# A two-layer hybrid encoder on Trainium2: gates after the second input tile, a normalisation without a DRAM turn, and three DMA queues

## The chip, the cores and the metric

The kernel runs on one core of a Trainium2 chip. The metric is the device time of one launch in microseconds (us). TensorE (PE) does the matrix products and transposes, VectorE (DVE), ScalarE (ACT) and GpSimd (POOL) do element-wise work, and DMAs are issued from an engine's own instruction stream: SyncE (SP) does nothing else, ACT and POOL issue them between their other instructions. PE writes its results to eight PSUM banks of 128 x 512 fp32.

## The reference

The input has 1024 tokens of width 1024; 16 learned tokens are put in front, so every activation is 1040 tokens long. Two layers follow, each a mixer and a SwiGLU FFN, with residual sums. The part that matters here is how the mixer gets its queries, keys, gates and decays:

```python
def l2norm(x):
    return x * lax.rsqrt(jnp.sum(x * x, axis=-1, keepdims=True) + L2_EPS)

def hybrid_mixer(h, ...):
    proj = h @ w_in
    qkv, z, b_raw, a_raw, sc_b, sc_c, sc_h = jnp.split(proj, idx, axis=-1)
    qkv = jax.nn.silu(depthwise_conv_centred(qkv, conv_qkv_w))
    q, k, v = jnp.split(qkv, 3, axis=-1)
    q = l2norm(q.reshape(Bsz, L, 4, 128))
    k = l2norm(k.reshape(Bsz, L, 4, 128))
    beta = jax.nn.sigmoid(b_raw).reshape(Bsz, L, 2, 4)
    g = -jnp.exp(a_log) * jax.nn.softplus(a_raw.reshape(Bsz, L, 2, 4) + dt_bias)
    o_fwd = chunk_gated_delta_rule(q, k, v, g[:, :, 0], beta[:, :, 0])
    o_bwd = flip(chunk_gated_delta_rule(flip(q), flip(k), flip(v), ...))
    ...
    y_sc = sc_b * depthwise_conv_centred(sc_c * sc_h, sc_conv_w)
    return jnp.concatenate([o * silu(z) ..., y_sc], axis=-1) @ w_out
```

Inside `chunk_gated_delta_rule` each chunk forms products of keys with keys and keys with queries, multiplies them by decays (exponentials of differences of the running sum of g), solves a triangular system, and a scan over the chunks carries a 128 x 128 state per head, forwards and backwards.

## The kernel before

**Layout.** Activations lie with features on the 128 partitions and tokens along the row: a tensor of 512 features is a tile `[128, 4, 1040]`. Every dense product is done in three matmuls for each 128 x 128 block of weights: high part by high part, high by low, low by high (L150, L151, L152 in `dense`). The weights arrive as fp32 (`raw`, L122, on SP's queue, 256 KB a transfer), ACT makes their high part `whi` (L123), and POOL, for some tiles DVE, their low part `wlo` (L124). There are three buffers each of `whi` and `wlo` and two of `raw`, so the next weights are fetched and split while PE works on the present ones.

**Order.** The program is written as straight Python loops for a scheduler that gives each instruction a priority and fixes one order for each engine before the run; `at_prio` moves parts of the code up or down. On the chip each engine follows its list and waits for semaphores. "Place" below means an instruction's position in that list of one engine. The list of SP holds all DMAs of the program, so a DMA that waits holds those behind it. Transfers also rotate over eight semaphores: each waits for the transfer eight before it on its kind of queue.

**A layer, in the order of the code:**

1. Input tiles (L405 to L434). `pos` 0 to 3 are the four heads of the keys (weight tiles 4 to 7), `pos` 4 to 7 those of the queries (tiles 0 to 3). Each tile is a dense product of 1024 x 128 weights with the 1040 tokens in three pieces `FULL` of 346 to 348 columns, a three-tap convolution, a SiLU and a square. The squares of a head are summed over their 128 features on PE, with a selecting matrix that puts head q into row q of a 32-row group, one group for each piece of columns (L425, bank `l2`).
2. `gates()` (L299), called at `pos == 6`, that is, at the third tile of the queries. It loads the small weights of beta and g, multiplies (L311, 48 matmuls), turns the result into tokens-on-partitions (L316), takes sigmoid and softplus through a chain of some 30 short DVE and ACT operations, sums g along the chunk on PE (L357, L358), transposes the sums (L361) and stores them to DRAM as `gd` (L364, on SP). It works in the tile `P0` (L305), and in three PSUM banks from `pa()`, which is a pool of one bank.
3. `normalise` (L376), for the keys behind `pos == 3` (with the tile `P1`) and for the queries behind `pos == 7` (with `P0`). The sums of four heads lie in 4 partitions by 1040 columns. ACT takes three square roots (L381), SP stores them to the DRAM buffer `rnd` (L382) and loads them back as 104 x 40 (L386), DVE takes the reciprocal (L387), SP stores it (L388), and for each head SP loads one row to all 128 partitions (L391) and DVE multiplies (L392). The tile for the queries is the `P0` that `gates` works in, so this load waits until the gates are done with it.
4. `k_out` (L394) transposes the keys and stores them for the scan (`vkd`, L403); value tiles follow, with transposes and stores in `v_store` (L463, L470, L472). Behind them stand the short convolution's twelve tiles and the four of z. Their matmuls have a low priority (`mmp`, `low`): they fill PE wherever the following parts leave room.
5. The chunk loop (L532): for each of nine chunks the products of keys with keys and with queries (L538, L539, banks `f` and `b`), for each direction a load of the rows of `gd` to all partitions (`gr`, L543), exponentials on ACT (L548, L552), products on DVE (L556, L560), a store for the scan (L562).
6. The triangular solve: 32 x 32 blocks on DVE and POOL (L603, L604), then joined on PE (L627 to L653).
7. The scan (`scan_step`, L673), nine chunks forwards and nine backwards, with dense filler between; then the output product and the FFN (L883 on).

Of the kernel before, what the change touches and what calls it, by code (L numbers as in the profile page):

```python
# [10 lines left out]
AF = mybir.ActivationFunctionType  # L11
# [7 lines left out]
H = 4  # L19
# [14 lines left out]
FULL = [(0, 348), (348, 694), (694, 1040)]  # L34
# [6 lines left out]
def trunk(ctx: ExitStack, tc: tile.TileContext, xT, w_in, w_ba, w_out, w_gu, w_dn,  # L41
          par_d, alog_d, dtb_d, cst_d, eye_d, out):
    nc = tc.nc
# [25 lines left out]
    def pa():  # L69
        return bank("a")  # L70
# [29 lines left out]
    ts = nc.vector.tensor_scalar  # L100
    ptt = nc.gpsimd.tensor_tensor
    dma = nc.sync.dma_start


    par = sb.tile([128, P_W], F32, name="par")
# [147 lines left out]
    for l in range(DEPTH):  # L253
# [45 lines left out]
        def gates():  # L299
# [7 lines left out]
            for (n0, n1) in FULL:  # L307
# [2 lines left out]
                    for j in range(2):  # L310
                        mm(ps[0:32, :n1 - n0], wb[:, k, :], x[k][j][:, n0:n1], start=(k == 0 and j == 0), stop=(k == 7 and j == 1))  # L311
                tt(out=bat[0:32, n0:n1], in0=ps[0:32, :n1 - n0], in1=rstd[0:32, n0:n1], op=ALU.mult)
            ps = pa()
            for c in range(9):
                s0 = 0 if c == 0 else 16 + 128 * (c - 1)
                mm(ps[:, c * 16:(c + 1) * 16], bat[0:32, s0:s0 + 128], sel2, start=True, stop=True)  # L316
# [34 lines left out]
            for d in range(2):  # L351
                tt(out=g[:, d], in0=sv[0][:, 36 * d:36 * d + 36].rearrange("p (c h) -> p c h", c=9),
                   in1=nA[:, 4 * d:4 * d + 4].unsqueeze(1).to_broadcast([128, 9, 4]), op=ALU.mult)
                ts(out=g[:, d, 0, :], in0=g[:, d, 0, :], scalar1=mask16, scalar2=None, op0=ALU.mult)
            psG = pa()
            for d in range(2):
                mm(psG[:, 36 * d:36 * d + 36], (utri, ltri)[d], fl(g)[:, 36 * d:36 * d + 36], start=True, stop=True)  # L357
            mm(psG[:, 72:144], ones, fl(g), start=True, stop=True)  # L358
            ts(out=fl(negG), in0=psG[:, 0:72], scalar1=-1.0, scalar2=None, op0=ALU.mult)
            psT = pa()  # L360
            nc.tensor.transpose(psT[0:72, 0:128], fl(negG), ident)  # L361
            grows = gt[0:72, 2, 0:128]
            nc.vector.tensor_copy(grows, psT[0:72, 0:128])
# [12 lines left out]
        def normalise(dst, l2, r, tag):  # L376

            scale, bias = ((float(HD), epsq), (1.0, epsc))[r > 0]
            r4 = row(Y[1] + "f")[0:4]
            for j, (n0, n1) in enumerate(FULL):  # L380
                act(out=r4[:, n0:n1], in_=l2[32 * j:32 * j + 4, :n1 - n0], func=AF.Sqrt, scale=scale, bias=bias[32 * j:32 * j + 4])  # L381
            dma(rnd[r:r + 4], r4)  # L382

            flat = rnd[r:r + 4].rearrange("a (b c) -> (a b) c", c=40)
            r104 = row(Y[1] + "f")[0:104, 0:40]
            dma(r104, flat)  # L386
            nc.vector.reciprocal(out=r104, in_=r104)  # L387
            dma(flat, r104)  # L388
            bc = big(tag)
            for h in range(H):  # L390
                dma(bc[:, h, :], rnd[r + h].partition_broadcast(128))  # L391
                tt(out=dst[:, h, :], in0=dst[:, h, :], in1=bc[:, h, :], op=ALU.mult)  # L392

        def k_out(c):  # L394

            n = 16 if c == 0 else 128
            s0 = 0 if c == 0 else 16 + 128 * (c - 1)
            ps = pa()
            for h in range(H):
                nc.tensor.transpose(ps[0:n, h * 128:(h + 1) * 128], KTt[:, h, s0:s0 + n], ident)  # L400
            kt = t2k("kt")
            act(out=kt[0:n].rearrange("p a b -> p (a b)"), in_=ps[0:n], func=AF.Copy)
            dma(vkd[c, 0:n, 1, :], kt[0:n].rearrange("p a b -> p (a b)"))  # L403

        for pos, i in enumerate((4, 5, 6, 7, 0, 1, 2, 3)):  # L405
            hh = pos % 4
            if hh == 0:
                l2, squares = None, []
            t = trow()
            late = pos < (2, 1)[l]  # L410
            inproj(i, to_row_late(t) if late else to_row(t), pfirst if l == 0 and pos == 1 else None)
            if late:
                tt(out=t, in0=t, in1=rstd, op=ALU.mult)
            dst = (QT if i < 4 else KTt)[:, hh, :]
            conv(t, dst, P_CV + 3 * i)
            act(out=dst, in_=dst, func=AF.Silu)
            act(out=t, in_=dst, func=AF.Square)

            squares.append((hh, t))
            if l > 0 or pos > 0:  # L420
                if l2 is None:
                    l2 = bank("f")
                for (q, sq_) in squares:
                    for j, (n0, n1) in enumerate(FULL):
                        mm(l2[32 * j:32 * j + 32, :n1 - n0], sel[:, 3 - q:35 - q], sq_[:, n0:n1], start=(q == 0), stop=(q == 3), skip_group_check=True)  # L425
                squares = []
            if pos == 6:
                beta, g, negG, negE, gl, bkd = gates()
            if pos == 3:
                normalise(KTt, l2, 4, "P1")  # L430
            if pos == 5:
                for c in range(9):
                    k_out(c)
# [24 lines left out]
        def v_store(i, v):  # L458

            for c0 in (0, 1, 5):  # L460
                ps = pa()
                if c0 == 0:
                    low(lambda: nc.tensor.transpose(ps[0:16, 0:128], v[:, 0:16], ident))  # L463
                    nc.vector.tensor_copy(vm[0:16, i, :], ps[0:16, 0:128])
                    if i == 3:
                        dma(vkd[0, 0:16, 0, :], vm[0:16].rearrange("p a b -> p (a b)"))
                else:
                    vt = v[:, 16 + 128 * (c0 - 1):16 + 128 * (c0 + 3)]
                    for c in range(4):
                        low(lambda: nc.tensor.transpose(ps[:, c * 128:(c + 1) * 128], vt[:, 128 * c:128 * c + 128], ident))  # L470
                    act(out=vt, in_=ps, func=AF.Copy)
                    dma(vkd[c0:c0 + 4, :, 0, i * 128:(i + 1) * 128].rearrange("c p e -> p c e"), vt.rearrange("p (c e) -> p c e", c=4))  # L472

        v = None
        for i in range(4):
# [56 lines left out]
        for c in range(9):  # L532
            n = 16 if c == 0 else 128
            s0 = 0 if c == 0 else 16 + 128 * (c - 1)
            kqp = [bank("fb"[c % 2]) for _ in range(2)]
            for h in range(H):
                o = (h % 2) * 256
                mm(kqp[h // 2][0:n, o:o + n], KTt[:, h, s0:s0 + n], KTt[:, h, s0:s0 + n], start=True, stop=True)  # L538
                mm(kqp[h // 2][0:n, o + 128:o + 128 + n], KTt[:, h, s0:s0 + n], QT[:, h, s0:s0 + n], start=True, stop=True)  # L539
            for d in (dirs0 if c == 0 else (0, 1)):  # L540
                pn[0] += 1
                gr, dt_, eg = pts[pn[0] % 4], pts[4 + pn[0] % 2], pts[6 + pn[0] % 2]
                dma(gr[:, :, 0:n], gd[36 * d + 4 * c:36 * d + 4 * c + 4, 0:n].partition_broadcast(128))  # L543
                aq = c4k("aq")
                at = aq[:, 0:512].rearrange("p (h i) -> p h i", h=4)
                qd = aq[:, 512:1024].rearrange("p (h i) -> p h i", h=4)
                if c > 0 or d == 1:
                    act(out=eg[:, :, 0:n], in_=gr[:, :, 0:n], func=AF.Exp, scale=-1.0)  # L548
                    tt(out=qd0 if c == 0 else qd, in0=QT[:, :, s0:s0 + n], in1=eg[:, :, 0:n], op=ALU.mult)
                ptt(out=gr[0:n, :, 0:n], in0=gr[0:n, :, 0:n], in1=off[0:n, d, 0:n].unsqueeze(1).to_broadcast([n, 4, n]), op=ALU.add)  # L550
                for h in range(H):
                    act(out=dt_[0:n, h, 0:n], in_=gr[0:n, h, 0:n], func=AF.Exp, scale=-1.0, bias=negG[0:n, d, c, h:h + 1])  # L552
                for j in range(2):
                    qk = kqp[j].rearrange("p (a b i) -> p a b i", a=2, b=2)[0:n, :, 1, 0:n]
                    o_ = at0[d][:, 2 * j:2 * j + 2, :] if c == 0 else at[:, 2 * j:2 * j + 2, :]
                    tt(out=o_, in0=qk, in1=dt_[0:n, 2 * j:2 * j + 2, 0:n], op=ALU.mult)  # L556
                for h in range(H):
                    o = (h % 2) * 256
                    dst = P0[d][:, h, :] if c == 0 else Pv[d][:, (c - 1) * 4 + h, :]
                    stt(out=dst, in0=kqp[h // 2][0:n, o:o + n], scalar=beta[0:n, d, c, h:h + 1], in1=dt_[0:n, h, 0:n], op0=ALU.mult, op1=ALU.mult)  # L560
                if c > 0:
                    dma(aqd[c, d].rearrange("p a b -> p (a b)"), aq[:, 0:1024])  # L562
                else:

                    Wm, Zm, Tm = mts
                    dma(m0d[d, 0].rearrange("h j i -> j h i"), P0[d])
                    dma(Wm, m0d[d, 0])
                    dma(Zm, eye_d[0:4, :, :][:, 0:16, 0:16])
                    for s in (range(15, 0, -1) if d == 0 else range(0, 15)):
                        r0, r1, a0, a1 = (0, s, s, 16) if d == 0 else (s + 1, 16, 0, s + 1)  # L570
                        sh = [4, r1 - r0, a1 - a0]
                        ptt(out=Tm[:, r0:r1, a0:a1], in0=Wm[:, r0:r1, s:s + 1].to_broadcast(sh), in1=Zm[:, s:s + 1, a0:a1].to_broadcast(sh), op=ALU.mult)
                        ptt(out=Zm[:, r0:r1, a0:a1], in0=Zm[:, r0:r1, a0:a1], in1=Tm[:, r0:r1, a0:a1], op=ALU.subtract)
                    dma(m0d[d, 1], Zm)
                    dma(P0[d], m0d[d, 1].rearrange("h j i -> j h i"))
# [677 lines left out]
```

## Time and profile before

| | before |
|---|---|
| timed executions | 2670.06, 2680.13, 2682.99 us |
| median | 2680.13 us |
| the profiled execution's own time | 2667.47 us |
| its span | 2665.7 us |
| mean granted PE clock over it | 0.983 |
| layer 0: tiles of keys, queries and the first of values | 50 to 174 us |
| layer 0: chunk loop; solve; scan | 174 to 250; 250 to 336; 336 to 560 us |
| layer 1: the same four | 1350 to 1517; 1517 to 1594; 1594 to 1670; 1670 to 1900 us |

The span runs from the first to the last instruction; the profiled execution's time is 1.8 us more. Times of instructions are microseconds from the span's start. The windows of the table were cut by hand where one stage's main instructions give way to the next stage's; the filler runs across these cuts. In a row of a timeline the columns are start, duration, engine, line, operation and the program's names of the destination and the source, with a count where several run back to back, and in brackets how long the engine was idle before and what ended that. In a row of a group they are line, engine, operation, names, count, shortest, median and longest duration in ns, and the start of the first and of the last in us. "SPq" is SP's queue of DMA issues: the duration is that of the issue, not of the transfer. Names such as `P`, `b`, `pf` stand for a tile's tag without its number: `P` is `P0` or `P1`, `pa`, `pf`, `pb`, `pacc` are PSUM banks.

### The profile page before, as it was taken

The page shows a single profiled execution, that of the slowest core. Times are in us where ns is not written, and L with a number is a line of the kernel's source. Part 1 is how long each engine was busy: PE and PEld are TensorE (multiplying, and loading weights), DVE is VectorE, ACT ScalarE, POOL GpSimd, SP SyncE. Part 2 cuts the span into 40 slices and gives each one's busy share as a digit, 9 for nine tenths or more (in the row PEclk, how much of TensorE's full clock was granted, in tenths as well). Part 3 has the DMA queues.
Part 4 walks back from the last instruction along what each step waited for, and adds up shares of the span by engine and source line. Part 5 has one row for each costly group of instructions (what it writes and reads, how often), then busy time and mean ns, then how long its engine had stood idle before and what let it go on. Part 6 is the DMA issues. An engine that isn't in the chain of part 4 may idle for free. (4 is left out here: it accounts for less than half of the span.)

```text
span 2665.7 us, 43982 instructions
## 1 busy us (share of the span) xinstructions
PE 2563.4 (96%) x17242; PEld 2346.7 (88%) x17242; DVE 1502.8 (56%) x2258; ACT 1032.8 (39%) x1932; POOL 1185.1 (44%) x922
## 2 busy tenths in 40 slices
PE   8998899999999999999999989999989999999997
PEld 7898899998999999999998977898877888887886
DVE  7369713548766566522353688135587766754216
ACT  5466334535333333321244662535343333332224
POOL 4136611224766666533221346112367666663342
PEclk9999889999999999999999999999999999999998
DMA  3246135634312222532222461356332222225321
GB/s 118 98 148 201 49 103 185 193 105 135 104 60 84 80 73 76 198 111 65 76 92 86 125 229 50 125 179 230 99 124 93 68 82 77 87 88 185 93 81 64
DMA packets 163491, 301.03 MB, mean 113 GB/s; under 512 B 20352, under 2 KB 57140, under 8 KB 163284
## 3 DMA queue, kind: packets, MB, share of 16 engines
q1 hardware_dynamic: 163284, 298.23, 34.2%
q8 instruction: 135, 2.21, 0.4%
q14 instruction: 72, 0.59, 0.1%
HBM read 222.99 MB, written 75.18 MB: 112 GB/s over the span
## 5 line engine op out<-in xcount | busy, mean ns | idle before, releaser
L124 POOL TENSOR_TENSOR wlo<-raw,whi 128x512 fp32r<-128x512 f32 x236 | 285.8, 1214 | 927.9 <-ACT whi L123 812.1
L150 PE MATMUL pacc<-a,whi 128*128 128x346 f32 (+2 forms) x1031 | 350.0, 342 | 10.6 <-ACT whi L123 6.1
L152 PE MATMUL pacc<-a,wlo 128*128 128x346 f32 (+2 forms) x1031 | 351.0, 342 | 6.8 <-DVE wlo L124 6.7
L123 ACT ACTIVATE whi<-raw 128x512 fp32r<-128x512 f32 (+2 forms) x264 | 151.7, 578 | 478.9 <-PE pacc L151 300.6
L151 PE MATMUL pacc<-a,whi 128*128 128x346 f32 (+2 forms) x916 | 313.2, 342 | 1.8 <-DVE a L799 1.7
L152 PE MATMUL pacc<-b,wlo 128*128 128x346 f32 (+2 forms) x882 | 303.3, 345 | 8.2 <-DVE wlo L124 8.2
L150 PE MATMUL pacc<-b,whi 128*128 128x346 f32 (+2 forms) x882 | 305.5, 347 | 4.2 <-ACT whi L123 2.1
L151 PE MATMUL pacc<-b,whi 128*128 128x346 f32 (+2 forms) x776 | 268.6, 347 | 0.7 <-DVE b L799 0.6
L150 PEld LDWEIGHTS pacc<-a,whi 128*128 128x128 f32 x1031 | 199.0, 194 | 21.7 <-ACT whi L123 6.5
L152 PEld LDWEIGHTS pacc<-a,wlo 128*128 128x128 f32 x1031 | 199.7, 194 | 16.5 <-DVE wlo L124 8.0
L151 PEld LDWEIGHTS pacc<-a,whi 128*128 128x128 f32 x916 | 177.3, 194 | 10.6 <-DVE a L799 2.0
L150 PEld LDWEIGHTS pacc<-b,whi 128*128 128x128 f32 x882 | 168.2, 191 | 20.1 <-issue 4.2
L152 PEld LDWEIGHTS pacc<-b,wlo 128*128 128x128 f32 x882 | 168.1, 191 | 19.2 <-DVE wlo L124 9.5
L942 POOL TENSOR_TENSOR wlo<-rw,whi 128x512 fp32r<-128x512 f32 x92 | 135.5, 1475 | 71.2 <-ACT whi L941 65.6
L151 PEld LDWEIGHTS pacc<-b,whi 128*128 128x128 f32 x776 | 147.9, 191 | 11.2 <-DVE b L799 1.6
L942 POOL TENSOR_TENSOR a<-rw,a 128x512 fp32r<-128x512 f32 x64 | 107.1, 1676 | 66.5 <-ACT a L941 66.4
L942 POOL TENSOR_TENSOR b<-rw,b 128x512 fp32r<-128x512 f32 x64 | 90.5, 1418 | 83.9 <-ACT b L941 52.3
L804 DVE TENSOR_TENSOR a<-pacc,a 128x346 f32<-128x346 f32 (+2 forms) x116 | 57.7, 500 | 108.3 <-PE pacc L152 107.1
L941 ACT ACTIVATE whi<-rw 128x512 fp32r<-128x512 f32 x92 | 58.0, 632 | 140.1 <-DVE rw L1015 72.5
L804 DVE TENSOR_TENSOR b<-pacc,b 128x512 f32<-128x512 f32 (+1 forms) x88 | 52.6, 599 | 99.2 <-PE pacc L152 98.9
L1011 DVE TENSOR_TENSOR rw<-rw,rw 128x512 f32<-128x512 f32 x44 | 68.5, 1556 | 49.3 <-POOL wlo L942 31.0
L1016 DVE TENSOR_TENSOR rw<-raw,rw 128x512 f32<-128x512 f32 x44 | 95.3, 2165 | 1.2
(822 smaller groups left out, 7504.3 us busy)
## 6 DMA issues: line engine op xcount, KB each, us to landing
raw<-in_w_in SPq DMA_DIRECT2D x112, 256.0 KB
raw<-in_w_gu SPq DMA_DIRECT2D x104, 256.0 KB
rw<-in_w_gu SPq DMA_DIRECT2D x88, 256.0 KB
aqd<-aq SPq DMA_DIRECT2D x32, 512.0 KB
rec<-aqd SPq DMA_DIRECT2D x62, 256.0 KB
rec<-vkd SPq DMA_DIRECT2D x61, 256.0 KB
raw<-in_w_dn SPq DMA_DIRECT2D x60, 256.0 KB
raw<-in_w_out SPq DMA_DIRECT2D x48, 256.0 KB
```

The costliest lines, as they stand in the source:

```text
L123: act(out=hi, in_=raw[:, 0:kk, :], func=AF.Copy)
L124: (tt if lov[0] else ptt)(out=lo, in0=raw[:, 0:kk, :], in1=hi.bitcast(F32), op=ALU.subtract)
L150: mm(ps[:, :n], wh, xh[:, n0:n1], start=(k == 0), stop=False)
L151: mm(ps[:, :n], wh, xl[:, n0:n1], start=False, stop=False)
L152: mm(ps[:, :n], wl, xh[:, n0:n1], start=False, stop=(k == K - 1))
L804: tt(out=hr[m][:, n0:n1], in0=ps, in1=hr[m][:, n0:n1], op=ALU.add)
L941: act(out=hi, in_=src, func=AF.Copy)
L942: ptt(out=lo, in0=src, in1=hi.bitcast(F32), op=ALU.subtract)
L1011: tt(out=s1t, in0=A21, in1=A22, op=ALU.add)
L1016: tt(out=A21, in0=A11, in1=A21, op=ALU.subtract)
```

## The change

There are three parts.

- The gates are called at `pos == 2`, the third tile of the keys, and their three PSUM banks come from the pool `b` of two banks, which the chunk loop and the solve use later.
- `normalise` sums the squares in four groups of 260 columns, so that they fill the 128 partitions in four groups of 32. One square root and one reciprocal work on 128 x 260 in place. Each head's four pieces are then stored to its row of `rnd` and loaded to all partitions by DMAs that POOL issues (`qdma`): eight a call, 32 in all.
- The stores of the transposed keys (18) and values (16) and the loads of the gates' rows (35) are issued by ACT (`adma`) instead of SP.

All else is the same source; the scheduler makes its lists anew.

```diff
@@ -102,2 +102,4 @@
     dma = nc.sync.dma_start
+    adma = nc.scalar.dma_start
+    qdma = nc.gpsimd.dma_start
 
@@ -312,3 +314,3 @@
                 tt(out=bat[0:32, n0:n1], in0=ps[0:32, :n1 - n0], in1=rstd[0:32, n0:n1], op=ALU.mult)
-            ps = pa()
+            ps = bank("b")
             for c in range(9):
@@ -354,3 +356,3 @@
                 ts(out=g[:, d, 0, :], in0=g[:, d, 0, :], scalar1=mask16, scalar2=None, op0=ALU.mult)
-            psG = pa()
+            psG = bank("b")
             for d in range(2):
@@ -359,3 +361,3 @@
             ts(out=fl(negG), in0=psG[:, 0:72], scalar1=-1.0, scalar2=None, op0=ALU.mult)
-            psT = pa()
+            psT = bank("b")
             nc.tensor.transpose(psT[0:72, 0:128], fl(negG), ident)
@@ -378,15 +380,10 @@
             scale, bias = ((float(HD), epsq), (1.0, epsc))[r > 0]
-            r4 = row(Y[1] + "f")[0:4]
-            for j, (n0, n1) in enumerate(FULL):
-                act(out=r4[:, n0:n1], in_=l2[32 * j:32 * j + 4, :n1 - n0], func=AF.Sqrt, scale=scale, bias=bias[32 * j:32 * j + 4])
-            dma(rnd[r:r + 4], r4)
-
-            flat = rnd[r:r + 4].rearrange("a (b c) -> (a b) c", c=40)
-            r104 = row(Y[1] + "f")[0:104, 0:40]
-            dma(r104, flat)
-            nc.vector.reciprocal(out=r104, in_=r104)
-            dma(flat, r104)
+            r4 = row(Y[1] + "f")[:, 0:260]
+            act(out=r4, in_=l2[:, 0:260], func=AF.Sqrt, scale=scale, bias=bias)
+            nc.vector.reciprocal(out=r4, in_=r4)
+            for h in range(H):
+                qdma(rnd[r + h].rearrange("(a c) -> a c", a=4), r4.rearrange("(a b) c -> a b c", b=32)[:, h, :])
             bc = big(tag)
             for h in range(H):
-                dma(bc[:, h, :], rnd[r + h].partition_broadcast(128))
+                qdma(bc[:, h, :], rnd[r + h].partition_broadcast(128))
                 tt(out=dst[:, h, :], in0=dst[:, h, :], in1=bc[:, h, :], op=ALU.mult)
@@ -402,3 +399,3 @@
             act(out=kt[0:n].rearrange("p a b -> p (a b)"), in_=ps[0:n], func=AF.Copy)
-            dma(vkd[c, 0:n, 1, :], kt[0:n].rearrange("p a b -> p (a b)"))
+            adma(vkd[c, 0:n, 1, :], kt[0:n].rearrange("p a b -> p (a b)"))
 
@@ -423,6 +420,6 @@
                 for (q, sq_) in squares:
-                    for j, (n0, n1) in enumerate(FULL):
+                    for j, (n0, n1) in enumerate([(260 * j, 260 * j + 260) for j in range(4)]):
                         mm(l2[32 * j:32 * j + 32, :n1 - n0], sel[:, 3 - q:35 - q], sq_[:, n0:n1], start=(q == 0), stop=(q == 3), skip_group_check=True)
                 squares = []
-            if pos == 6:
+            if pos == 2:
                 beta, g, negG, negE, gl, bkd = gates()
@@ -471,3 +468,3 @@
                     act(out=vt, in_=ps, func=AF.Copy)
-                    dma(vkd[c0:c0 + 4, :, 0, i * 128:(i + 1) * 128].rearrange("c p e -> p c e"), vt.rearrange("p (c e) -> p c e", c=4))
+                    adma(vkd[c0:c0 + 4, :, 0, i * 128:(i + 1) * 128].rearrange("c p e -> p c e"), vt.rearrange("p (c e) -> p c e", c=4))
 
@@ -542,3 +539,3 @@
                 gr, dt_, eg = pts[pn[0] % 4], pts[4 + pn[0] % 2], pts[6 + pn[0] % 2]
-                dma(gr[:, :, 0:n], gd[36 * d + 4 * c:36 * d + 4 * c + 4, 0:n].partition_broadcast(128))
+                adma(gr[:, :, 0:n], gd[36 * d + 4 * c:36 * d + 4 * c + 4, 0:n].partition_broadcast(128))
                 aq = c4k("aq")
```

## The prediction

> **What bounds the kernel now.** I read the page first, then the busy times by stretch, then the waits of TensorE (PE), then the SP and VectorE (DVE) timelines around the normalisation of the queries. A line such as L391 is a line of the kernel before.
>
> ```profile
> span 2665.7 us, 43982 instructions
> ...
> PE 2563.4 (96%) x17242; PEld 2346.7 (88%) x17242; DVE 1502.8 (56%) x2258; ACT 1032.8 (39%) x1932; POOL 1185.1 (44%) x922
> ...
> q1 hardware_dynamic: 163284, 298.23, 34.2%
> ```
>
> PE is busy 96% of the span, so at most 102 us of idle can be won anywhere. All transfers of the program itself run on one hardware queue; none on a queue fed by GpSimd (POOL). The stretches, layer 0 and then layer 1, each as input tiles of K, Q and first V, then chunk loop, then block solve, then scan:
>
> ```profile
> core 0: us, PE busy (x) PEld busy (x) DVE busy (x) ACT busy (x) POOL busy (x), PEclk, DMA share, GB/s
> 50.00:174.00 124.00, 123.63 (x801) 113.43 (x800) 63.60 (x94) 65.15 (x84) 26.06 (x19) 0.99 0.30 96
> 174.00:250.00 76.00, 66.71 (x443) 63.95 (x444) 64.34 (x153) 49.96 (x112) 51.21 (x79) 0.98 0.68 219
> 250.00:336.00 86.00, 75.38 (x832) 72.30 (x831) 68.06 (x104) 32.31 (x41) 52.04 (x72) 0.92 0.20 68
> 336.00:560.00 224.00, 218.02 (x1795) 209.00 (x1792) 87.21 (x216) 97.48 (x292) 37.48 (x25) 0.95 0.49 159
> 1350.00:1517.00 167.00, 166.88 (x1065) 154.10 (x1063) 76.53 (x119) 77.64 (x102) 31.24 (x24) 0.99 0.28 92
> 1517.00:1594.00 77.00, 67.89 (x410) 61.82 (x409) 67.29 (x152) 54.82 (x115) 40.29 (x48) 0.98 0.68 218
> 1594.00:1670.00 76.00, 66.67 (x587) 56.48 (x587) 63.72 (x94) 22.12 (x28) 49.56 (x69) 0.93 0.17 56
> 1670.00:1900.00 230.00, 227.84 (x1890) 206.56 (x1885) 91.50 (x211) 98.39 (x284) 45.53 (x32) 1.00 0.50 162
> ```
>
> The stretch with the code that moves (50 to 174, and 1350 to 1517) has no idle to give: 0.37 and 0.12 us. In the chunk loops and solves PE loses 9.29 + 10.62 + 9.11 + 9.33 = 38.35 us, with DVE 79 to 87% busy; in the scans 5.98 + 2.16 us. What PE waits for from 160 to 350 is not the chain of the attention but its dense filler work:
>
> ```profile
> engine line waited for: us in total, times, longest us
> PE pacc L152 <- DVE wlo L124: 6.7, 3, 4.2
> PE pa L463 <- ACT b L471: 4.4, 1, 4.4
> PE pb L538 <- DVE P L560: 2.9, 3, 1.3
> ```
>
> The low parts of weights split on DVE, and copies of V, come late because they stand in DVE's and ACT's queues among the chunk loop and the solve. Only the third row belongs to the chain.
>
> **The wait that the change takes away.** SP's timeline around the query normalisation, in layer 0 (layer 1 has the same order):
>
> ```profile
> 147.75 0.30 SPq L388 DMA_DIRECT2D rnd<-b3f  x1
> 148.15 10.45 SPq L122 DMA_DIRECT2D raw<-in_w_in  x3
> 160.90 0.32 SPq L364 DMA_DIRECT2D gd<-P  x1
> 162.38 1.86 SPq L391 DMA_DIRECT2D P<-rnd  x4
> ```
>
> The reciprocal is stored at 147.75, but its broadcast leaves at 162.38, 1.48 us after the store of the gates (L364): it needs the buffer P0 that the gates hold, and stands behind them on SP. So gates after tile 2 release the broadcast, not the missing DRAM turn alone. PE did not stand still meanwhile (0.37 us idle).
>
> **Cost, part by part.** The last sums of squares of Q, the square roots with their table loads and a reciprocal over 128 by 260, each from the groups of its line:
>
> ```profile
> L425 PE MATMUL pf<-b,sel x48: 454/467/481, 62.9 to 138.2; 128*32 128x346 f32 x32, 128*32 128x348 f32 x16
> ```
>
> ```profile
> L381 ACT ACT_TABLE_LOAD  x4: 1283/1283/1283, 76.0 to 1481.0; - x4
> ...
> L381 ACT ACTIVATE b3f<-pf,epsq x3: 542/542/542, 140.2 to 141.3; 4x346 f32<-4x346 f32 x2, 4x348 f32<-4x348 f32 x1
> ```
>
> ```profile
> L192 DVE RECIPROCAL r<-r x3: 1740/1767/1778, 674.9 to 1984.8; 128x260 f32<-128x260 f32 x2, 128x256 f32<-128x256 f32 x1
> ```
>
> The products with the broadcast, from DVE's timeline:
>
> ```profile
> 166.45 3.50 DVE L392 TENSOR_TENSOR b<-b,P 128x1040 f32<-128x1040 f32 x2 [1.81 <-DMA P<-rnd]
> ...
> 170.90 2.38 DVE L392 TENSOR_TENSOR b<-b,P 128x1040 f32<-128x1040 f32 x2
> ```
>
> In the built order of the program before, these sums stand at PE's places 292 to 751, which is (138.2 - 62.9)/459 = 0.164 us a place. Let T be the end of the last of them, and p the time that POOL needs to issue one transfer. Normalisation: one square root instead of three (0.6 us, the table load ahead of it), a reciprocal of 1.77 us (nothing waits on DVE there: 63.60 of 124 us busy): T + 2.4. Then POOL in its built order: four stores, a low part, four broadcasts, a low part. The low parts of layer 0's stretch and what POOL waited for ahead of them, then the broadcasts' issues on SP:
>
> ```profile
> L124 POOL TENSOR_TENSOR wlo<-raw,whi x17: 1278/1289/2385, 50.3 to 166.4; 128x512 fp32r<-128x512 f32 x17
> ...
>   ACT whi L123: 101.1, 15
> ```
>
> ```profile
> L391 SPq DMA_DIRECT2D P<-rnd x16: 326/426/549, 84.2 to 1505.8; - x16
> ```
>
> The broadcasts leave from T + 2.4 + 4p + 1.3; the first lands 166.45 - 162.38 = 4.1 us later, and the fourth product ended 10.9 us after the issue (170.90 + 2.38 - 162.38). The trace has no POOL transfer. The nearest rows are an SP issue of 0.43 us below and a two-input POOL operation of 1.29 us, at its longest 2.4, above; I take p = 1, nearer the POOL operation, and 0.4 to 2.4 as its ends. Then the first query product begins at T + 11.8 = 150.0 instead of 166.45, and all end at T + 18.6 = 156.8 instead of 173.28: the chain starts 16 us earlier. PE's first query product moves from place 935 to 866, which is 69 places or 11.3 us; 109 places behind the sums it is reached at T + 17.9, so it hardly waits.
>
> What this does to PE is in the low parts behind the broadcasts. For Q the last is done at T + 2.4 + 4p + 1.3 + 4p + 1.3 = T + 5 + 8p, and PE needs it 69 places, 11.3 us, behind: 1.7 us late at p = 1, none at 0.79 and below, 12.9 at 2.4. For K there is the same sum, and the need comes 89 places, 14.6 us, behind: none at 1, 9.6 at 2.4. POOL waits for ACT 101 us in this stretch, so its time is free; its order is not. Both layers: 3.4 us, between 0 and 45.
>
> Gates: their matmuls move to places 220 to 267, before the fourth tile, with the same instructions and other PSUM banks. Before, no PE wait came of them. Their DVE chain:
>
> ```profile
> 138.00 0.20 DVE L329 COPY beta<-pa 128x36 f32<-128x36 f32 x1 [2.22 <-PE pa L316]
> ...
> 152.44 0.36 DVE L354 TENSOR_SCALAR g<-g,misc 128x4 f32<-128x4 f32 x2
> ```
>
> That is 14.8 us, with other tiles' work inside; PE now comes to the sums over g (L357) 68 places, 11.2 us, after the last L316. So 3.6 us late a layer at worst, 0 if less stands between: I take 1.5, 3.0 in all. The sums of squares go from three to four matmuls with the same 1040 columns: 4 x 0.467 x 260/346 = 1.40 = 3 x 0.467, nothing.
>
> ACT takes 69 transfers off SP (18 of K, 16 of V, 35 of the gate rows) and four table loads more (5.1 us). The same issues cost SP:
>
> ```profile
> L403 SPq DMA_DIRECT2D vkd<-kt x18: 319/327/1004, 100.0 to 1474.9; - x18
> ```
>
> ```profile
> L543 SPq DMA_DIRECT2D ptm<-gd x35: 319/338/2007, 164.3 to 1567.7; - x35
> ```
>
> At 0.33 us the 51 in the chunk loops are 8.4 us a layer on an ACT that is busy 49.96 of 76: hidden in its idle time. If that cover is gone, the V copies are later, and the 4.4 us wait of L463 grows. Every transfer also waits for the one eight before it in the built order, so ACT can now be held by SP's stores; SP in turn carries less. Nothing is charged for either, 19 us at the upper end (third rival).
>
> The head start I price at 2 us of gain, out of the 8.14 us of scan idle: filler remains behind the scan in the built order, and the chunk loop spans 311 places of PE after, 303 before, the solve starting 367 behind it against 372. So the crowding that makes the 38.35 us moves along with the chain. Sum: 3.4 + 3.0 - 2 = +4.4 us, 2671.9 on the profiled execution's own 2667.47. That execution lies 12.7 us under the median 2680.13 of the three timed ones; the middle of all four is 2675.1, so I predict 2680. About 0.5%, 13.4 us, is what a measurement can tell from no change.
>
> **Rivals.** *POOL is slow to issue.* One transfer takes p = 2, as DVE's two-input operations already stretch POOL's 1.29 us to 2.39. Then Q costs 21 - 11.3 = 9.7 and K 21 - 14.6 = 6.4 us a layer, 32 in all, and with the gates 2675 + 35 = 2710. It decides for slower from p = 1.3. For it: DVE is in use beside every transfer; against: 26.06 of 124 us of POOL are busy there. [...]
>
> *The chain gains what it starts earlier.* With 16 us more, DVE is less crowded from 174 to 336, and half of the 38.35 us of PE idle goes: -19 us, 2656. It decides from an idle of 25 us in the four stretches; with 27 us of it gone the time is 2648. For it: only 63.60 of 124 us of DVE are busy in the stretch into which the chain moves; against: the wait rows name filler.
>
> *ACT becomes the crowded queue.* Table loads, issues and waits hold V's copies, and the idle of the four stretches grows by half: +19 us, 2694.
>
> *Nothing moves:* the broadcasts still leave late, held by something else than the gates: 2675.
>
> **How the numbers follow.** Forecast 0.33, nothing moves 0.03, slow POOL 0.28, crowded ACT 0.10, gain 0.26. Faster by over 0.5%: 0.26; same: 0.36; slower: 0.38. The range runs from the gain's farther end, 2648, to the slow POOL at p = 2.3, which makes 12.1 + 8.8 us a layer and 2720; it leaves out under a tenth at each end, where p is over 2.3 or yet more of the idle goes. The forecast's own range is 2667 to 2693.
>
> **What would show it.** Right: the broadcasts of Q leave about 9 us after the last sum of squares, the first chunk product of Q comes 11 us or more earlier, PE waits under 3 us a layer for low parts on POOL, and the idle of the chunk loops and solves together stays near 38 us. Wrong: POOL's transfers of 1.4 us and more with PE waiting on wlo from POOL; an idle of those stretches under 25 or over 52 us; a granted clock there that differs by more than 0.03, which no step here foresees.

## The result and the profile after

Over 22 runs the changed kernel took 2691.81 us (median, 2676.84 to 2703.77), the kernel before 2677.24 us over 22 runs: a ratio of 1.0053, with a 95% interval of 1.0035 to 1.0071. It is slower by some 14 us; forecast was 2680, no change. The gates now stand behind the third input tile (`pos == 2`), not the second as the title has it, and the normalisation keeps one of its two turns through DRAM. Lines below are those of the changed kernel: up to the gates they stand 2 later than before, behind the normalisation 3 earlier.

The page of the changed kernel, its head and its queues:

```profile
span 2693.9 us, 43978 instructions
...
PE 2586.9 (96%) x17274; PEld 2365.8 (88%) x17274; DVE 1511.4 (56%) x2258; ACT 1034.5 (38%) x1928; POOL 1206.2 (45%) x954
...
q1 hardware_dynamic: 143004, 272.57, 30.8%
q10 hardware_dynamic: 17008, 16.95, 2.1%
q0 software_dynamic: 2816, 8.59, 1.0%
```

PE's idle time is 2693.9 - 2586.9 = 107.0 us, against 102.3 before. That is 4.7 us more, close to the 4.4 of the forecast's sum. But PE is also *busy* for 23.5 us longer, on nearly the same matmuls (32 more, of the sums of squares). The two profiles lie 28.2 us apart, twice as far as the medians: that of before is of one of its faster executions (clock 0.983, its mean is 0.9805), that of the changed kernel of one of its slower ones (0.972, its mean is 0.9754). The stretches show where the time went, in the windows of the prediction (length, busy times by engine, then the granted clock third from the right):

```profile
50.00:174.00 124.00, 122.78 (x830) 112.42 (x830) 72.77 (x119) 71.31 (x101) 40.04 (x44) 1.00 0.32 103
174.00:250.00 76.00, 65.67 (x419) 63.81 (x418) 61.90 (x137) 50.02 (x96) 45.53 (x73) 0.93 0.61 211
250.00:336.00 86.00, 73.13 (x814) 69.55 (x813) 63.28 (x92) 26.85 (x36) 51.38 (x66) 0.84 0.16 53
336.00:560.00 224.00, 221.18 (x1780) 215.25 (x1780) 85.50 (x212) 93.96 (x274) 41.46 (x28) 0.95 0.51 164
...
1350.00:1517.00 167.00, 165.69 (x1083) 153.00 (x1082) 86.47 (x135) 81.39 (x116) 44.79 (x44) 1.00 0.31 102
1517.00:1594.00 77.00, 65.71 (x417) 60.71 (x416) 64.75 (x151) 55.09 (x104) 37.53 (x50) 0.98 0.62 207
1594.00:1670.00 76.00, 67.62 (x557) 58.27 (x557) 63.05 (x90) 23.57 (x30) 47.45 (x65) 0.86 0.15 48
1670.00:1900.00 230.00, 225.75 (x1827) 204.17 (x1827) 82.09 (x195) 92.89 (x269) 43.90 (x29) 0.93 0.49 160
```

Busy time multiplied by the missing share of the clock is an estimate of what the clock costs. It is an upper one, since not all work takes twice as long at half the clock: in the test further down, 178 records of 32 by 32 matmuls took 2.84 us of busy time at a clock of 1.00 and 158 took 4.00 us at 0.50, which is 1.6 times as long for each. In the six rows from the chunk loops on the product is 4.6 + 11.7 + 11.1 + 1.3 + 9.5 + 15.8 = 54.0 us; the same sum from the rows of before is 1.3 + 6.0 + 10.9 + 1.4 + 4.7 + 0 = 24.3 us. The difference, 29.7 us, is more than the 23.5 us that PE was busy longer, but of its size.

Most of it lies where the blocks of the solve are joined on PE. These are the windows from the first join to the last, layer 0 and layer 1, first in the kernel before and then in the changed one:

```profile
306.70:385.30 78.60, 77.25 (x1114) 71.72 (x1114) 18.19 (x31) 37.59 (x62) 16.90 (x22) 0.83 0.22 73
1645.50:1712.40 66.90, 65.89 (x1059) 55.52 (x1059) 17.77 (x30) 35.57 (x55) 13.64 (x14) 1.00 0.25 82
```

```profile
299.10:377.30 78.20, 76.17 (x1059) 69.93 (x1059) 19.21 (x33) 34.28 (x53) 11.86 (x13) 0.72 0.17 54
1644.40:1731.60 87.20, 84.27 (x1052) 68.56 (x1052) 19.30 (x32) 36.08 (x55) 13.22 (x14) 0.77 0.18 59
```

PE is busy there 17.3 us longer with fewer records, and the product is 13.1 + 0 us before and 21.3 + 19.4 us after. The 1.00 of before is partly luck: the test kernel below begins with the code of the kernel before, and in its profile the joins of layer 1 run at 0.88:

```profile
1648.60:1722.50 73.90, 73.21 (x1060) 61.34 (x1059) 17.28 (x30) 35.65 (x55) 13.60 (x14) 0.88 0.23 75
```

How much of the 14 us is the clock can be read from all runs. The mean granted clock of the changed kernel's 22 runs is 0.9754, and that of 70 runs of the kernel before, taken beside the experiments, 0.9805. Within either kernel, runs with a clock lower by 0.01 took some 19 us longer (an estimate, from a straight line through each kernel's runs), so the 0.0051 are worth some 10 us. Where both kernels have runs at the same clock (between 0.974 and 0.982), the changed kernel's took on average some 5 us longer. That rest is of the size of the idle time that came on top, 4.7 us.

The moved code itself did nearly what was forecast. POOL's timeline at the queries' normalisation (start, duration, then in brackets the idle time ahead):

```profile
144.78 2.30 POOL L385 DMA_DIRECT2D rnd<-b3f  x4
147.10 1.30 POOL L126 TENSOR_TENSOR wlo<-raw,whi 128x512 fp32r<-128x512 f32 x1
148.55 1.12 POOL L388 DMA_DIRECT2D P<-rnd  x2
150.02 1.04 POOL L388 DMA_DIRECT2D P<-rnd  x2 [0.35 <-DMA rnd<-b3f]
```

The broadcasts leave at 148.55 instead of 162.38. PE's waits from 50 to 174 us are these two, and none is for a low part on POOL or for the gates:

```profile
PE pa L397 <- DVE b L389: 0.9, 1, 0.9
PE pf L422 <- ACT b L414: 0.2, 1, 0.2
```

From 174 to 336 us two waits have grown. The solve's first products (L624) wait 6.4 us for DVE's substitution, against 0.6 us before (L627 there). The transposes of V wait 7.9 us for ACT, against 4.4 us of L463 in the prediction's rows.

```profile
PE pa L460 <- ACT b3f L479: 5.0, 1, 5.0
PE pf L624 <- DVE b L604: 4.4, 1, 4.4
PE pa L460 <- ACT b L479: 2.9, 1, 2.9
PE pb L624 <- DVE b L604: 2.0, 1, 2.0
```

### The profile page after: what moved, and what is told of

It reads as the page before. It is cut to its first block, busy times and chain, and to the rows that moved or that the text cites. A ratio compares the mean times of both kernels' runs of the same rounds, so it can differ in the third digit from the quotient of the medians.

```text
span 2693.9 us, 43978 instructions
## 1 busy us (share of the span) xinstructions
PE 2586.9 (96%) x17274; PEld 2365.8 (88%) x17274; DVE 1511.4 (56%) x2258; ACT 1034.5 (38%) x1928; POOL 1206.2 (45%) x954
## 5 line engine op out<-in xcount | busy, mean ns | idle before, releaser
L152 PE MATMUL pacc<-a,whi 128*128 128x346 f32 (+2 forms) x1031 | 351.0, 343 | 9.4 <-ACT whi L125 6.4
L152 PE MATMUL pacc<-b,whi 128*128 128x346 f32 (+2 forms) x882 | 309.9, 352 | 7.1 <-ACT whi L125 3.7
L154 PE MATMUL pacc<-b,wlo 128*128 128x346 f32 (+2 forms) x882 | 309.7, 353 | 5.0 <-DVE wlo L126 5.0
L153 PE MATMUL pacc<-b,whi 128*128 128x346 f32 (+2 forms) x776 | 271.7, 351 | 0.6 <-DVE b L796 0.6
L152 PEld LDWEIGHTS pacc<-a,whi 128*128 128x128 f32 x1031 | 199.1, 194 | 21.2 <-ACT whi L125 6.6
L152 PEld LDWEIGHTS pacc<-b,whi 128*128 128x128 f32 x882 | 170.9, 194 | 21.5 <-ACT whi L125 4.5
```

The lines of the kernel that those rows point to most:

```text
L152: mm(ps[:, :n], wh, xh[:, n0:n1], start=(k == 0), stop=False)
L153: mm(ps[:, :n], wh, xl[:, n0:n1], start=False, stop=False)
L154: mm(ps[:, :n], wl, xh[:, n0:n1], start=False, stop=(k == K - 1))
```

## The experiments

"Clock" is the mean granted clock of a kernel's runs, "time x clock" the mean of their products; it would be the time at full clock if all of the time went with the clock, which by the 19 us for 0.01 it does only in part. Ratios are to runs of the kernel before on the same chip.

| kernel | us, median (runs) | ratio, 95% interval | clock | time x clock |
|---|---|---|---|---|
| before | 2677.0 (70) | 1 | 0.9805 | 2624 |
| the change | 2691.8 (22) | 1.0035 to 1.0071 | 0.9754 | 2624 |
| gates alone | 2713.2 (5) | 1.0104 to 1.0147 | 0.9736 | 2638 |
| normalisation alone, on POOL | 2643.1 (4) | 0.9856 to 0.9894 | 0.9832 | 2598 |
| ACT's queue alone | 2651.5 (6) | 0.9888 to 0.9925 | 0.9832 | 2606 |
| the change, all on SP | 2670.8 (12) | 0.9972 to 1.0009 | 0.9783 | 2614 |
| the change without its gates | 2665.9 (5) | 0.9940 to 0.9969 | 0.9786 | 2609 |
| that, broadcast of queries in P1 | 2665.1 (5) | 0.9935 to 0.9969 | 0.9792 | 2610 |
| gates alone, chain held | 2687.6 (8) | 1.0020 to 1.0058 | 0.9788 | 2632 |
| only the gates' banks | 2695.8 (5) | 1.0042 to 1.0078 | 0.9752 | 2627 |
| only the gates' place | 2705.1 (6) | 1.0079 to 1.0120 | 0.9752 | 2636 |
| the change, joins spread | 2680.0 (12) | 0.9999 to 1.0034 | 0.9777 | 2620 |
| before, joins together | 2650.3 (6) | 0.9885 to 0.9922 | 0.9847 | 2610 |
| the change, joins together | 2667.9 (12) | 0.9946 to 0.9984 | 0.9796 | 2612 |
| normalisation alone, joins together | 2642.6 (6) | 0.9839 to 0.9902 | 0.9855 | 2603 |
| normalisation alone, on SP | 2677.9 (12) | 0.9980 to 1.0024 | 0.9767 | 2614 |

**The parts alone.** Each is one part of the diff put into the kernel before: the gates with their banks, the normalisation with `qdma`, the three lines with `adma`. The fourth is the whole change with both queues back on SP:

```diff
-    adma = nc.scalar.dma_start
-    qdma = nc.gpsimd.dma_start
+    adma = nc.sync.dma_start
+    qdma = nc.sync.dma_start
```

> Gates alone: called behind the third tile of the keys, with banks of pool b; the normalisation and all queues as before. First theory (the lost clock comes with the chain's new place among the filler, which the gates alone set: first chunk product at PE's place 816 against 892 before and 812 in the changed kernel): slower than before by 8 to 16 us, with a mean granted clock 0.004 to 0.007 under that of before, and the busy time of PE longer while its idle time stays. Second theory (the loss comes from the transfers issued by POOL and ACT): within 4 us of before.

> The normalisation alone: four groups of 260 columns, reciprocal in place, stores and broadcasts issued by POOL; gates and the other queues as before. First theory: the broadcast of the queries still waits for the gates' buffer and the chain stays at its place (first chunk product at 903 against 892), so within 5 us of before. Second theory: POOL's transfers cost here as they do in the changed kernel, 5 to 10 us slower.

> The 69 transfers of keys, values and gate rows issued by ACT alone; all else as before. First theory: the chain stays (first chunk product at 892), within 5 us of before. Second theory: ACT's issues hold the copies of V and the exponentials, 5 to 10 us slower.

> The changed kernel with every transfer back on SP: gates after the third tile and the new normalisation, no queue on POOL or ACT. First theory: slower than before by 8 to 16 us like the changed kernel itself, with the same lower clock in the chunk loop and the solve. Second theory: within 4 us of before or faster.

Neither theory gave these numbers. The gates cost 34 us, the normalisation with POOL's queue gains 33 and ACT's queue 25. The queues, which the second theory blamed, gain. With all transfers on SP the change is level with the kernel before, the one result that the second theory had. The three add up to some 25 us of gain, and the whole change loses 14: the parts don't add. The pages' PE lines for gates alone and for the normalisation alone, whose spans are 2711.3 and 2644.8:

```profile
PE 2595.0 (96%) x17242; PEld 2368.8 (87%) x17242; DVE 1508.1 (56%) x2258; ACT 1040.8 (38%) x1937; POOL 1185.2 (44%) x922
```

```profile
PE 2551.2 (96%) x17274; PEld 2342.0 (89%) x17274; DVE 1503.7 (57%) x2258; ACT 1024.3 (39%) x1920; POOL 1196.6 (45%) x954
```

With the gates alone PE idles 116.3 us, 14 more than in the profile of before, and is busy 31.6 us longer on the same matmuls; with the normalisation alone it idles 93.6 and is busy 12.2 us less. By the 19 us for 0.01, the mean clock makes some 13 of the gates' 34 us and some 5 us of each of the two gains, so most of what the parts do alone is not the mean clock.

**Is it the early chain?** The chain of chunk loop and solve starts earlier with the gates. Four kernels set its place in other ways: the change without its gates; the gates alone with the broadcast of the queries tied to the second V tile; only the gates' banks changed; and the first of these with the broadcast in P1. Their edits, the first against the changed kernel, the second against the gates alone, the third against the kernel before, the last against the first:

```diff
-            ps = bank("b")
+            ps = pa()
...
-            if pos == 2:
+            if pos == 6:
```

```diff
-                dma(bc[:, h, :], rnd[r + h].partition_broadcast(128))
+                after(dma(bc[:, h, :], rnd[r + h].partition_broadcast(128)), hold)
...
+            if i == 1:
+                normalise(QT, l2, 0, "P0", held[2])
```

```diff
-            ps = pa()
+            ps = bank("b")
...
```

```diff
-        normalise(QT, l2, 0, "P0")
+        normalise(QT, l2, 0, "P1")
```

> The change without its gates: the new normalisation with POOL's transfers and the ACT queue, gates behind the third tile of the queries and in pool a as before; first chunk product at PE's place 903. Place theory (an early chain costs clock and idle time, the other two parts gain): their gains of 32 and 24 us add up in part, 2615 to 2640 us, granted clock 0.982 or more. Rival (POOL's and ACT's queues disturb each other, as the parts do not add up in the changed kernel): no better than the better of the two alone, 2640 to 2660.

> The gates alone as in the first experiment (behind the third tile of the keys, pool b), with the broadcast of the queries held back by an added dependency on the second tile of V, so that the chain starts later: first chunk product at place 866, against 816 with the gates alone and 892 before. Place theory: about a third of the loss is left, 2680 to 2695 us. Rival (the gates' own work ahead of the fourth tile of the keys costs): 2705 to 2715 as with the gates alone.

> Only the three banks of the gates come from pool b, the gates stay behind the third tile of the queries, normalisation and queues as before. The built order has the chain early all the same: first chunk product at place 818 instead of 892. Place theory: 2700 to 2715 us, clock 0.970 to 0.977, like the gates alone. Rival (the early gates cost): 2668 to 2682, as before.

> The kernel of the first of these four with the broadcast of the queries in tile P1 instead of P0, so that it no longer waits for the gates: first chunk product at place 811 instead of 903, gates where they were before. Place theory: 15 to 35 us slower than that kernel, with a clock of 0.970 to 0.978. Rival (the early gates cost, not an early chain): within 5 us of that kernel, or faster.

Held back, the gates cost 10 us instead of 34, and the banks alone, which bring the chain to place 818 with the gates where they were, cost 16, more than the rival allows and less than the place theory asks. Both speak for the place. But with the broadcast in P1 the chain stands at 811 and the time and the clock are those of the kernel it was made from, 2665. In this pair an early chain costs nothing, and the place theory falls as a rule. The change without its gates is 26 us faster than the change and slower than either of its two parts alone, outside the ranges of both theories.

**What lowers the clock.** Test stretches behind the end of the kernel before, each begun by 40 full matmuls (128 by 128, 346 columns) that bring the clock to 1.00 (0.50 from 2686 to 2690 us and 1.00 from 2694, ahead of the first stretch):

```python
for run, fill, times in ((512, 0, 1), (32, 1, 14), (32, 2, 12), (32, 4, 10), (32, 8, 8), (64, 16, 4)):
    ...
    for g_ in range(times):
        for i in range(run):
            p_small(i)
        for i in range(fill):
            p_dense()
```

> The kernel before with a test of TensorE's clock put behind its end; the test's products are not used. Ten stretches, each begun with 40 full matmuls (128 by 128 weights, 346 columns): 512 matmuls of 32 by 32 alone; runs of 32 such with 1, 2, 4 and 8 full ones after each run; runs of 64 with 16 full ones; 384 matmuls of 64 by 64 alone; full ones in runs of 12 behind one, two and three short VectorE operations that PE must wait for. Joins theory (an array that is busy with small matmuls alone counts as idle for the clock): the granted clock goes to 0.50 in the stretches of small matmuls alone and of 1 or 2 full ones, and stays over 0.95 with 8 and with 16. Gap theory (only idle time lowers it): the clock stays at 1.00 in all stretches of small matmuls, and falls only behind the waits.

The stretches by time, in one run. A small fp32 matmul leaves two records (4352 for the test's 2176 of 32 by 32). The first row holds the last 401 of the 512 small matmuls alone, and the others follow in the order of the list, then 64 by 64 alone, then the three with waits:

```profile
2696.50:2717.60 21.10, 18.77 (x802) 18.34 (x802) 0.00 (x0) 0.00 (x0) 0.00 (x0) 0.65 0.02 5
2726.80:2755.60 28.80, 27.83 (x910) 23.74 (x910) 0.00 (x0) 0.00 (x0) 0.00 (x0) 0.68 0.02 4
2764.70:2785.60 20.90, 19.89 (x770) 16.62 (x771) 0.00 (x0) 0.00 (x0) 0.00 (x0) 0.98 0.02 4
2794.50:2814.00 19.50, 19.50 (x670) 16.98 (x670) 0.00 (x0) 0.00 (x0) 0.00 (x0) 1.00 0.02 4
2822.50:2842.00 19.50, 19.50 (x527) 17.61 (x520) 0.00 (x0) 0.00 (x0) 0.00 (x0) 1.00 0.01 3
2850.00:2866.00 16.00, 16.00 (x495) 15.18 (x488) 0.00 (x0) 0.00 (x0) 0.00 (x0) 1.00 0.02 4
2874.00:2898.00 24.00, 24.00 (x778) 23.72 (x777) 0.00 (x0) 0.00 (x0) 0.00 (x0) 1.00 0.02 4
2905.00:2922.00 17.00, 13.94 (x81) 12.53 (x80) 2.60 (x5) 0.00 (x0) 0.00 (x0) 1.00 0.00 0
2931.00:2946.00 15.00, 9.89 (x55) 8.76 (x56) 4.55 (x9) 0.00 (x0) 0.00 (x0) 1.00 0.00 0
2954.00:2977.00 23.00, 12.88 (x72) 11.21 (x72) 8.79 (x17) 0.00 (x0) 0.00 (x0) 1.00 0.00 1
```

With 32 by 32 matmuls alone, PE is busy for 18.77 of 21.10 us and the clock falls all the same, to a mean of 0.65. One full matmul behind each 32 does not hold it (0.68); two hold it for some 20 us and lose it at the end of their stretch (0.98); four and more hold it throughout. Waits that leave PE idle 44% of the time, in pieces of some 1.7 us, leave it at 1.00. So the joins theory holds in its kind, though not in its numbers: two full matmuls had been expected to give 0.50, and 64 by 64 alone, which had been expected to fall too, stays at 1.00 once the clock is up. The gap theory fails in its claim that only idle time lowers the clock. Two longer waits lowered it too; those of the test, between full matmuls, are of some 1.7 us at most. In the changed kernel the wait for L624 is one: PE idles for 4.41 us behind full matmuls, and within it the clock goes to 0.50.

```profile
294.70:298.00 3.30, 0.02 (x1) 0.00 (x0) 3.00 (x7) 0.00 (x0) 2.88 (x6) 0.99 0.00 0
298.00:299.20 1.20, 0.06 (x2) 0.07 (x4) 1.20 (x2) 0.00 (x0) 0.48 (x2) 0.50 0.00 0
...
299.14 1.06 PE L624 MATMUL pf<-b,P 32*32 32x32 f32 x32 [4.41 <-DVE b L604]
```

The kernel before has such a wait too, 4.15 us for a low part (L152) that ends at 294.17, and its clock is 0.50 from 293 to 294. So the clock fell in two settings here, in waits of 4.41 and 4.15 us and, in the test, in stretches of small matmuls (a mean of 0.65), and the runs of the kernels don't part them in full.

**The joins in the kernels.** Two edits touch only the order among the solve's joins (L624 to L650) and behind, and a third kernel is for the question of the pool. The first gives each group of joins a place among the filler; the second, one line, lets the two directions' joins alternate; the third kernel moves the gates and leaves their banks in pool a.

```diff
+            slot = [0]
...
+            def spread(f):
+                here = tc.cur_priority
+                at_prio(base + 1000000 + 700 + 4 * d + 8 * slot[0])
+                slot[0] += 1
+                f()
+                at_prio(here)
...
```

```diff
-            at_prio(base - 20000 + 1000 * d)
+            at_prio(base - 20000)
```

> The changed kernel with one more edit: the groups of small matmuls that join the solve's blocks take priorities among the dense filler, so that the built order has 178 and 181 dense matmuls between the first and the last of them (layer 0, layer 1) instead of 139 and 132; everything ahead of the solve stands as in the changed kernel. Joins theory (little filler among the small matmuls lets the clock fall): mean clock 0.979 to 0.984, 2665 to 2684 us. Gap theory (the clock falls because of the waits in the chunk loop and ahead of the solve, which are the same here): clock 0.973 to 0.977, 2686 to 2698 us, as the changed kernel.

> The kernel before with one edit: both directions' joins have the same priority, so that fewer dense matmuls stand between them (151 and 121 instead of 186 and 139), with no gates, normalisation or queue changed and everything ahead of the solve in the same order. Joins theory: clock 0.973 to 0.977, 2684 to 2696 us. Gap theory: 2668 to 2682 us, clock as before.

> Gates behind the third tile of the keys, but with their banks from pool a as before; normalisation and queues as before. The chain is early (810) and 135 and 158 dense matmuls stand among the joins. Joins theory: clock 0.973 to 0.978, 2683 to 2700 us. Rival (it is pool b, which the chunk loop and the solve need, that costs): 2668 to 2682 us as before.

Spreading the joins won back 12 of the changed kernel's 14 us, with nothing ahead of the solve touched, though its clock, 0.9777, is below the range of the joins theory. The gates' place without pool b costs 27 us, 5 more than the upper end of the range, so the loss does not need that pool. But the kernel before with joins together was to be slower, and it is 26 us faster: it has less filler among its joins and more clock. The count of filler is therefore not the measure; the stretch is also over sooner, 56.3 us instead of 78.6 from the first join of layer 0 to the last. Nor is the gain the clock alone: the 0.0042 make some 8 of the 26 us, and in layer 1 the joins take 60.1 us at a clock of 0.91 with the line and 66.9 us at 1.00 without, with 121 and 139 full matmuls among them. The last runs put the same line into the changed kernel and into the normalisation alone, and the normalisation on SP:

> The changed kernel with the one edit that made the kernel before faster: the joins of both directions at the same priority. The gates, the banks, the normalisation and the queues are those of the change, and so is the built order up to the solve. Joins theory (the changed kernel loses its time because its joins run at half the clock): 2655 to 2678 us, clock 0.980 to 0.985. Rival (its loss lies in the chunk loop and ahead of the solve, which this leaves alone): 2684 to 2698 us.

> The normalisation alone with POOL's transfers (the fastest part of the change) with the joins of both directions at the same priority. If the two gains (33 and 28 us) are of different stages, 2610 to 2630 us; if both are only the joins' clock, 2640 to 2650 us.

> The normalisation alone with its stores and broadcasts on SP instead of POOL; gates and other queues as before. If the new form of the normalisation brings the 33 us of the second experiment: 2640 to 2655 us. If POOL's queue does (it orders the broadcasts otherwise): 2665 to 2685. By the joins theory the clock lies between, since 147 and 155 full matmuls stand among the joins instead of 188 and 177 with POOL's queue: 0.976 to 0.981.

The changed kernel with this line takes 2667.9 us, 24 less than without, and is faster than the kernel before too. But the line is worth 26 us to the kernel before as well. With joins together in both kernels the change still costs 17.6 us (2667.9 against 2650.3), and the clocks are as far apart as without the line (0.9796 against 0.9847). So the line does not take back what the change does; it is a gain of its own that both kernels have. Its PE line (span 2659.6):

```profile
PE 2553.5 (96%) x17274; PEld 2339.8 (88%) x17274; DVE 1511.3 (57%) x2258; ACT 1031.5 (39%) x1926; POOL 1206.3 (45%) x954
```

PE idles 106.1 us, as in the changed kernel (107.0), and is busy 33.4 us less. The windows of the joins in layer 0, of the changed kernel and then of this one:

```profile
332.00:340.00 8.00, 8.00 (x74) 7.14 (x73) 0.00 (x0) 1.77 (x3) 0.00 (x0) 0.50 0.01 2
340.00:348.00 8.00, 8.00 (x97) 7.15 (x96) 0.00 (x0) 2.95 (x5) 0.00 (x0) 0.50 0.01 2
348.00:356.00 8.00, 8.00 (x128) 7.40 (x127) 0.52 (x1) 2.94 (x5) 0.00 (x0) 0.50 0.35 109
```

```profile
332.00:340.00 8.00, 8.00 (x102) 7.12 (x101) 0.52 (x1) 0.61 (x2) 0.00 (x0) 0.58 0.00 0
340.00:348.00 8.00, 8.00 (x160) 7.68 (x156) 0.00 (x0) 5.21 (x9) 0.00 (x0) 1.00 0.02 4
348.00:356.00 8.00, 8.00 (x130) 7.65 (x127) 0.52 (x1) 3.70 (x7) 0.00 (x0) 1.00 0.01 2
```

PE is busy all the time in both; from 340 to 348 us it gets through 160 records at a clock of 1.00 and through 97 at 0.50. The two gains of normalisation and joins are mostly the same time, 2642.6 with both and 2643.1 with the normalisation alone. And the normalisation in its new form but on SP gains nothing: what gains is POOL's queue, or the built order that comes with it. The fastest kernels of the study are the normalisation alone on POOL, with or without the line.

## Why the prediction was wrong

- **POOL's issue.** p was taken as 1 us between 0.4 and 2.4. The stores took 0.57 us and the broadcasts 0.54 (medians; 0.75 the longest):

```profile
L385 POOL DMA_DIRECT2D rnd<-b3f x8: 563/572/752, 96.8 to 146.5; - x8
```

```profile
L388 POOL DMA_DIRECT2D P<-rnd x16: 527/540/587, 99.9 to 1500.4; - x16
```

  By the prediction's own threshold (none late at 0.79 and below) the 3.4 us charged for low parts are 0, and no such wait is in the rows. The slow-POOL rival fell. The landing of the broadcasts took 7.1 us in the median.
- **Head start.** The first product of keys with queries came at 158.8 instead of 169.5, 10.7 us earlier: just short of the 11 that were to show it right, and of the 16 of the sum. The broadcasts' issue was faster than priced, but the last sums came at 141.4 instead of 138.2, and the first broadcast landed 5.9 us after its issue instead of 4.1 (the product with it, L389, starts at 154.42).
- **The gates' chain.** 3.0 us were charged; no wait of it is in the rows.
- **Sum of idle time.** 4.4 us forecast, 4.7 measured, which is luck: the two terms that were charged are absent, the scans' idle time fell by 1.1 us instead of 2, and the growth of the L624 and L460 waits stands in their place. In the chunk loops and solves the idle time is 42.87 us, inside the bounds given.
- **The step that failed.** "So the crowding that makes the 38.35 us moves along with the chain": the sum let the clock of those stretches move along unchanged, a term put at nothing without a reason. It fell from 0.92 to 0.84 and from 0.93 to 0.86 in the solves, which is the sign of error that the prediction named, and from 0.83 to 0.72 and from 1.00 to 0.77 between the first join and the last. That term, some 10 of the 14 us by all runs, was left out of the sum and has no rival; the other 5 us are of the size of the idle time, which the sum had by luck. The rows of before already showed that the clock is no constant: 0.92 and 0.93 in the solves against 1.00 in layer 1's scan, with PE 88% busy in the solves.
- **ACT's queue.** Nothing was charged, and its rival was a loss of 19 us. Alone it gains 25, of which no step spoke. In the whole change the wait that the rival named, for V's transposes, did grow, by 3.5 us in layer 0.

Shown is that the change lowers the granted clock (0.9754 against 0.9805), that most of what this costs lies among the joins (PE is busy there 17.3 of the 23.5 us longer), that 32 by 32 matmuls alone lower the clock (to 0.50, with PE busy for 18.77 of 21.10 us), and that the order of the joins moves clock and time, in both kernels alike. Not shown is by which step the change lowers it. Each of the edits also changes the order that the scheduler builds, and the two were not told apart. Open as well: what makes the larger part of what gates, normalisation, ACT's queue and the line do alone, which is not the mean clock; why the gates alone add 14 us of idle time, why POOL's and ACT's queue together give up most of their gains; how much of the kernels' lost clock comes from waits like those of 4.41 and 4.15 us and how much from the small matmuls; and which property of the order among the joins counts, since the count of filler does not.

## What to carry to other kernels

Put the granted clock into the sum as a term of its own: busy time by the missing share of the clock, for each stretch, as an upper estimate, and ask of an edit whether a stretch of small matmuls will stand otherwise among the large ones. Where a scheduler builds the order, parts of a change need not add, so one part alone tells little of the whole. Compare runs at the same clock before putting a difference down to the work. And try an edit in the old kernel as well as in the new: a gain that both have explains nothing of the difference between them. Among the joins of the changed kernel PE was busy for all of 24.00 us (332 to 356) at a clock of 0.50, and letting the two directions' joins alternate was worth 24 and 26 us here.

## What the runs showed of the hardware

From a clock of 1.00, 32 by 32 matmuls alone brought it to 0.50 some 6.4 us after the first of them (2696.4 to 2702.8 in the test), although PE was 89% busy in their window; four full matmuls behind every 32 held it for the 19.5 us of the test, and 64 by 64 alone held it for 24 us. Waits of some 1.7 us between full matmuls left it at 1.00; a wait of 4.41 us in the changed kernel and one of 4.15 us in the kernel before took it to 0.50. DMA issues cost POOL 0.54 us (L388) and 0.57 us (L385) each in the median, against 0.33 on ACT in the same kernel (L540, 0.327).
